# A modulation product moved from TensorE columns to VectorE half rows in a two-block transformer kernel

## The chip, the cores and the metric

One core of a Trainium2 chip runs the whole program. The metric is the device time of one execution in microseconds (us), as the median of several executions; lower is better. The engines of the core are called PE (TensorE, the matrix engine; PEld is its weight load), DVE (VectorE), ACT (ScalarE), POOL (GpSimd) and SP (SyncE, whose queue issues nearly all DMA transfers). Each engine executes its own list of instructions in order and waits for the others by semaphores.

## The reference, cut to what matters

The program computes two transformer blocks of two layers each, on 256 tokens with 1024 features; the first block also carries 256 context tokens through its first layer. In the first block each layer has an adaptive modulation: two condition vectors (`c` for the tokens, `c_ctx` for the context) give six vectors of 1024 numbers each, which shift, scale and gate what the layer does. The change concerns only this product, for the second layer (`l = 1`).

```python
for l in range(DEPTH):                                   # DEPTH = 2
    want_ctx = l < DEPTH - 1
    mod_x = jax.nn.silu(c) @ ada_w[l] + ada_b[l]         # ada_w[l]: 1024 x 6144, float32
    mod_c = jax.nn.silu(c_ctx) @ ada_w[l] + ada_b[l]
    sh1, sc1, g1, sh2, sc2, g2 = jnp.split(mod_x[:, None, :], 6, axis=-1)
    sh1c, sc1c, g1c, sh2c, sc2c, g2c = jnp.split(mod_c, 6, axis=-1)
    hx = rmsnorm(x, norm1_w[l]) * (1.0 + sc1) + sh1
    hc = rmsnorm(xc, norm1_w[l]) * (1.0 + sc1c) + sh1c
    mix_x, mix_c = token_mixers(hx, hc, ...)
    x = x + g1 * mix_x
    hx = rmsnorm(x, norm2_w[l]) * (1.0 + sc2) + sh2
    x = x + g2 * conv_ffn(hx, ...)
    if want_ctx:                                         # not in the last layer
        xc = xc + g1c * mix_c
        ...
```

In the second layer the context only enters through `sh1c` and `sc1c` (parts 0 and 1); its other four parts are not used.

## The kernel before

Features lie on the 128 partitions, tokens along the rows. A matrix of 1024 input features is cut into 8 blocks of 128 (`KD` = 8). Every large product is done with split operands: a float32 value is written as a rounded high part and a low part, and three matmuls (high-high, high-low, low-high; lines 414 to 416) give one block product. The weights arrive as 512 KB transfers of eight 128x128 blocks (`load`, line 344, five buffers in this stage); ACT rounds the high part (line 323), DVE subtracts to get the low part (line 307, tile `wl`), and four buffers of split weights stand between these two and PE.

The modulation of layer 1 is computed inside the feed-forward stage of layer 0 (`conv_ffn`), beside its matmuls. That stage has two halves. Each half first makes 11 pairs of up-projection products of 512 columns (`lin`, 8 blocks, 24 matmuls of 512 columns each; PE pays for two such products per pair), which ACT and DVE turn, by a short convolution, a Silu and a split (tiles `t`, `ah`, `al`), into the input of the down-projection; then 8 down-projection products of 11 blocks (33 matmuls), each followed by two DVE instructions that add into the residual (`residual`, line 724). Three accumulators in PSUM (tile `mm`) are used in turn.

Side work is cut into steps by Python generators. `queue(name, interval, depth, gens)` registers them; after each product `lin` calls `tick(us)` with the product's nominal time, `kt * 3 * columns / 2400` us (5.12 us for an up-projection, 7.04 us for a down-projection), and one step is taken for each `interval` of credit. `flush` takes all steps that are left. `soon()` raises the priority of what is traced in it, and `issue_after(ins)` puts instructions behind `ins` on its engine. From priorities and dependencies a scheduler fixes the order of every engine's instruction list when the program is built.

`ada_group` (line 595) is the generator for the modulation. One group covers 2048 of the 6144 columns. For each of 16 pieces it loads 512 KB (`araw`, one buffer, its transfer placed behind the last weight transfer) and does four matmuls with the two condition vectors as a stationary operand of 32 columns (line 605; float32, so each is two instructions, eight in all), which collect in four partition strips of one PSUM bank. At the end ACT copies the bank, PE transposes it in four pieces (line 614) and DVE adds the bias into `mod`. Layer 1 has three such groups, queued at an interval of 7.0 us at the start of the feed-forward stage of layer 0.

At the end of the stage comes a chain that PE waits for: the last residual, sums of squares over features (line 490), a power on POOL, a transposed spread (line 499), and `modnorm`, in which DVE, ACT and POOL make the input of layer 1. `warm` puts filler matmuls (line 369) into PE's wait.

Of the kernel before, what the change touches and what calls it, by code (L numbers as in the profile page):

```python
# [22 lines left out]
F32 = mybir.dt.float32  # L23
# [6 lines left out]
P = 128  # L30
D = 1024
# [257 lines left out]
class _K:  # L289
    def __init__(self, ctx, tc, a):  # L290
        self.ctx, self.tc, self.nc, self.a = ctx, tc, tc.nc, a
        self.queues = {}
        self.extra, self.wturn = None, [0, 0]
        self.last_load = None
        self.nsplit, self.held = 0, None
        self.last_mm = None
        self.ada1 = False

# [4 lines left out]
    def stt(self, out, in0, s, in1, op0, op1):  # L303
        self.nc.vector.scalar_tensor_tensor(out, in0, s, in1, op0=op0, op1=op1)  # L304

    def tt(self, out, in0, in1, op):
        self.nc.vector.tensor_tensor(out, in0, in1, op=op)  # L307
# [14 lines left out]
    def split(self, h, l, src):  # L322
        self.nc.scalar.copy(h, src)  # L323
        self.tt(l, src, h.bitcast(F32), OP.subtract)
# [201 lines left out]
    def setup(self):  # L526
# [23 lines left out]
        self.mod = [c.tile([P, 48, 2], F32, name=f"mod{l}") for l in range(DEPTH)]  # L550

# [68 lines left out]


# [22 lines left out]
    def modnorm(self, l, scale, part_shift, segs, xs, rb):  # L644

        shift = self.mod[l][:, part_shift * 8:(part_shift + 1) * 8, :]
        with self.soon():
            for k in range(KD):
# [10 lines left out]
                self.tt(xs[1][:, k, :nq], w, xs[0][:, k, :nq].bitcast(F32), OP.subtract)  # L659
# [13 lines left out]
    def block1(self, l, parts):  # L673
# [4 lines left out]
        with ExitStack() as lay:  # L678
# [7 lines left out]
            with ExitStack() as ph:  # L686
# [5 lines left out]
                else:  # L692
                    self.more_weights(ph, f"wm{l}", 0, 1)
                    rb = self.token_scale(parts)
                    if not self.ada1:
                        with tc.tile_pool(name="ada1", bufs=1) as ap:
                            for g in range(3):
                                for _ in self.ada_group(1, g, ap, 16):
                                    pass
# [8 lines left out]
            with ExitStack() as ph:  # L708
                self.more_weights(ph, f"wf{l}", 2, 2)
                if l == 0:  # L710
                    self.ada1 = True
                    self.queue("ada", 7.0, 1, *[self.ada_group(1, g, ada) for g in range(3)])
# [6 lines left out]
    def residual(self, ps, n, gate, l, segs, parts=None):  # L719

        g = self.mod[l][:, gate * 8:(gate + 1) * 8, :]
        for i, s in enumerate(segs):
            x = self.x[s][:, n, :]
            self.stt(x, ps[:, i * 256:(i + 1) * 256], g[:, n, 1 - s:2 - s], x, OP.mult, OP.add)
# [17 lines left out]
    def conv_ffn(self, l, st, xs, segs, nq):  # L742
# [8 lines left out]
        with tc.tile_pool(name=f"ffn{l}", bufs=1) as fp:  # L751
            for hf in range(halves):
                a_ = (fp.tile([P, nh, nq], F32R, name="ah"), fp.tile([P, nh, nq], F32R, name="al"))
                ready = []
                for jj in range(nh):
                    j = hf * nh + jj
                    if not ready:
                        banks = [self.tiles(nq) for _ in range(2 if hf + jj == 0 else G % 2 + 1)]
                        if hf + jj == 0:
                            self.lins(banks, st["wup"], xs, cols)  # L760
                        ready = [ps for bank in banks for ps in bank]
# [4 lines left out]
                    with self.soon():  # L766
# [13 lines left out]
                        self.split(a_[0][:, jj, :], a_[1][:, jj, :], v)  # L780
                parts = self.out(st["wdn"], a_, nh, 5, l, segs, hf == halves - 1)
        return parts
# [938 lines left out]
```

## Time and profile before

| | us |
|---|---|
| median of 3 runs | 3097.07 (3096.97 to 3097.26) |
| the profiled execution | 3097.39 |
| its span, first to last instruction | 3095.7 |
| PE busy | 3047.0 (98% of the span) |
| DVE busy | 1866.6 (60%) |
| ACT busy | 1468.1 (47%) |
| POOL busy | 405.5 (13%) |

The profile is of one execution. The share of busy time is an average over stages; what a change in one stage is worth is read from that stage. A "busy" matmul is pipelined with its neighbours, so the time that PE pays for it is the distance from its start to the next start, not its duration. "Idle before" an instruction is time in which its engine had nothing to run, with what ended it.

### The profile page before, as it was taken

Reading aid. Unit: us, or ns where it says so; the run is one execution under the profiler, and the core shown is the slowest. Engines: PE = TensorE matmul, PEld = TensorE weight load, DVE = VectorE, ACT = ScalarE, POOL = GpSimd, SP = SyncE. Lnnn points to the kernel's source line nnn. Section 1 sums busy time; section 2 is a strip of 40 time slices with the busy share of each in tenths; the row PEclk is TensorE's granted clock in tenths of the full one; section 3 lists DMA queues with packets and bytes.
Section 4 is the critical chain, followed back from the end, with each engine's and each line's share of the span. In section 5 each row is a group of like instructions: output and inputs, shape, how many; then the busy total and the mean of one; then the engine's idle time right before and its main releaser. Section 6 shows DMA issues by size and latency. Waiting matters only on the chain.

```text
span 3095.7 us, 52954 instructions
## 1 busy us (share of the span) xinstructions
PE 3047.0 (98%) x21412; PEld 2745.8 (89%) x21412; DVE 1866.6 (60%) x3064; ACT 1468.1 (47%) x2414; POOL 405.5 (13%) x419
## 2 busy tenths in 40 slices
PE   6999999999999999999999999999999999999999
PEld 4777878887777778899999999999999999999999
DVE  4467864336535546776587565576665665676664
ACT  4344463324323335455465444655544544654543
POOL 3212130112000033211100100122000000121000
PEclk9999999999999999999999999999999999999999
DMA  7423212324444423225555555444455554444553
GB/s 247 145 93 127 78 68 96 109 96 144 156 141 145 150 89 104 76 93 175 184 187 180 184 185 184 143 149 151 161 193 185 169 185 162 150 153 157 171 184 116
DMA packets 163429, 453.98 MB, mean 147 GB/s; under 512 B 14832, under 2 KB 66288, under 8 KB 162672
## 3 DMA queue, kind: packets, MB, share of 16 engines
q1 hardware_dynamic: 162464, 449.11, 43.9%
q8 instruction: 168, 2.75, 0.4%
q10 hardware_dynamic: 720, 1.49, 0.1%
q14 instruction: 77, 0.63, 0.1%
HBM read 447.13 MB, written 1.05 MB: 145 GB/s over the span
## 4 chain that ended last, share of the span: by engine, by line
PE 96%; DMA 1%; DVE 1%; ACT 1%; SPq 0%; issue 0%; POOL 0%; DVEq 0%; ACTq 0%; POOLq 0%
PE mm L414 25%; PE mm L416 25%; PE mm L415 25%; PE mm L436 2%; PE aux L605 2%; PE mm L437 2%; PE mm L435 2%; PE mm L428 1%; PE mm L429 1%; PE mm L427 1%; PE aux L1068 1%; DMA araw<-in_ada_dram 1%; PE aux L369 1%; PE aux L1569 1%; PE aux L1053 1%; PE aux L1043 1%
## 5 line engine op out<-in xcount | busy, mean ns | idle before, releaser
L307 DVE TENSOR_TENSOR wl<-raw,wh 128x1024 fp32r<-128x1024 f32 x746 | 922.2, 1239 | 780.9 <-ACT wh L323 763.0
L323 ACT CAST wh<-raw 128x1024 fp32r<-128x1024 f32 x746 | 782.5, 1051 | 1074.1 <-PE mm L415 736.4
L414 PE MATMUL mm<-xh,wh 128*128 128x256 f32 (+1 forms) x3680 | 1144.3, 311 | 4.2 <-ACT ao L301 3.0
L415 PE MATMUL mm<-xl,wh 128*128 128x256 f32 (+1 forms) x3680 | 1143.4, 311 | 0.0
L416 PE MATMUL mm<-xh,wl 128*128 128x256 f32 (+1 forms) x3680 | 1142.8, 311 | 0.0
L414 PEld LDWEIGHTS mm<-xh,wh 128*128 128x128 f32 x3680 | 699.3, 190 | 47.4 <-issue 8.4
L415 PEld LDWEIGHTS mm<-xl,wh 128*128 128x128 f32 x3680 | 699.5, 190 | 43.1 <-issue 9.6
L416 PEld LDWEIGHTS mm<-xh,wl 128*128 128x128 f32 x3680 | 699.3, 190 | 42.5 <-issue 7.5
L416 PE MATMUL mm<-ah,wl 128*128 128x256 f32 (+1 forms) x1056 | 317.5, 301 | 0.2 <-DVE wl L307 0.2
L415 PE MATMUL mm<-al,wh 128*128 128x256 f32 (+1 forms) x1056 | 317.6, 301 | 0.0
L414 PE MATMUL mm<-ah,wh 128*128 128x256 f32 (+1 forms) x1056 | 316.9, 301 | 0.0
L415 PEld LDWEIGHTS mm<-al,wh 128*128 128x128 f32 x1056 | 200.9, 190 | 9.1 <-issue 2.5
L416 PEld LDWEIGHTS mm<-ah,wl 128*128 128x128 f32 x1056 | 200.9, 190 | 9.1 <-issue 2.1
L414 PEld LDWEIGHTS mm<-ah,wh 128*128 128x128 f32 x1056 | 200.6, 190 | 8.7 <-issue 2.1
L310 POOL TENSOR_TENSOR small<-small,mhalf 128x2 f32<-128x2 f32 (+2 forms) x48 | 50.6, 1054 | 1051.7 <-DVE small L304 713.2
L310 POOL TENSOR_TENSOR ss<-ss,t 128x256 f32<-128x256 f32 (+1 forms) x68 | 72.1, 1061 | 623.7 <-ACT t L301 602.3
L304 DVE SCALAR_TENSOR_TENSOR cv<-glu,p,cv 128x512 f32<-128x512 f32 (+1 forms) x240 | 150.7, 628 | 3.5
L414 PE MATMUL mm<-bh,wh 128*128 128x512 f32 (+1 forms) x384 | 129.0, 337 | 1.3 <-ACT wh L323 0.7
L416 PE MATMUL mm<-bh,wl 128*128 128x512 f32 (+1 forms) x384 | 129.0, 337 | 0.3 <-DVE wl L307 0.3
L415 PE MATMUL mm<-bl,wh 128*128 128x512 f32 (+1 forms) x384 | 129.2, 337 | 0.0
L436 PE MATMUL mm<-wh,xl 128*128 128x256 f32 x448 | 127.8, 287 | 0.0
L437 PE MATMUL mm<-wl,xh 128*128 128x256 f32 x448 | 127.4, 286 | 0.0
(331 smaller groups left out, 4283.8 us busy)
## 6 DMA issues: line engine op xcount, KB each, us to landing
araw<-in_ada_dram SPq DMA_DIRECT2D x96, 512.0 KB, 3.9
raw<-in_a_wup_dram SPq DMA_DIRECT2D x88, 512.0 KB, 3.4
raw<-in_b_f1u_dram SPq DMA_DIRECT2D x88, 512.0 KB, 3.4
raw<-in_b_f2u_dram SPq DMA_DIRECT2D x88, 512.0 KB, 3.4
raw<-in_a_wi_dram SPq DMA_DIRECT2D x78, 512.0 KB, 3.3
raw<-in_b_wb_dram SPq DMA_DIRECT2D x72, 512.0 KB, 3.3
raw<-in_b_wi_dram SPq DMA_DIRECT2D x48, 512.0 KB, 3.4
raw<-in_a_wdn_dram SPq DMA_DIRECT2D x44, 512.0 KB, 3.3
```

Of the source, the lines that this page charges most:

```text
L304: self.nc.vector.scalar_tensor_tensor(out, in0, s, in1, op0=op0, op1=op1)
L307: self.nc.vector.tensor_tensor(out, in0, in1, op=op)
L310: self.nc.gpsimd.tensor_tensor(out, in0, in1, op=op)
L323: self.nc.scalar.copy(h, src)
L369: self.last_mm = self.nc.tensor.matmul(ps[0:32], x, x[:, 0:1].to_broadcast([P, 256]), start=True, stop=True).ins
L414: mm(ps, h, xh[:, k, cols], start=k == 0, stop=False)
L415: mm(ps, h, xl[:, k, cols], start=False, stop=False)
L416: self.last_mm = mm(ps, l, xh[:, k, cols], start=False, stop=k == kt - 1).ins
L435: mm(ps, xh, w[0], start=start, stop=False)
L436: mm(ps, xl, w[0], start=False, stop=False)
L437: mm(ps, xh, w[1], start=False, stop=stop)
L605: nc.tensor.matmul(ps[32 * j:32 * j + 32, c * 256:(c + 1) * 256], self.cpad[:, k, :], raw[:, j, :], start=k + c == 0, stop=k + c == KD)
```

## The change

The three groups of layer 1 are replaced by a generator `ada_parts`, which goes through the six parts of 1024 columns one after the other. For each block of 128 rows it loads 128x1024 numbers (512 KB, `arow`, four buffers, three transfers ahead), and DVE multiplies each row by the condition's value of that row and adds it to an accumulator of 128x1024, in two halves of 512. A part is closed by four PE transposes per half, a DVE sum along rows and the addition of the bias. The context's vector is done for parts 0 and 1 only; the rest of `mod` is set to zero once at the start. Each DVE instruction is placed behind the latest split or residual on DVE (`pace`). The generator is queued after the first up-projections, without raised priority, with an interval of 3.8 us during the up-projections and 1.4 us during the down-projections. The scratch pool `ada1` (four `arow`, two accumulators) is opened for the feed-forward stage. Layer 0 keeps `ada_group`.

```diff
@@ class _K
+        self.pace = None
     def stt(self, out, in0, s, in1, op0, op1):
-        self.nc.vector.scalar_tensor_tensor(out, in0, s, in1, op0=op0, op1=op1)
+        return self.nc.vector.scalar_tensor_tensor(out, in0, s, in1, op0=op0, op1=op1).ins
...
         self.mod = [c.tile([P, 48, 2], F32, name=f"mod{l}") for l in range(DEPTH)]
+        nc.gpsimd.memset(self.mod[-1], 0.0)
...
+    def ada_parts(self, l, parts, pool):
+        nc = self.nc
+        H = D // 2
+        src = [(part, k) for part in parts for k in range(KD)]
+        raws = {}
+
+        def fetch(i):
+            if i < len(src):
+                part, k = src[i]
+                raws[i] = pool.tile([P, D], F32, name="arow", bufs=4)
+                nc.sync.dma_start(raws[i], self.a["ada"][l, k * P:(k + 1) * P, part * D:(part + 1) * D])
+
+        for i in range(3):
+            fetch(i)
+        yield
+        for i, (part, k) in enumerate(src):
+            sets = (0,) if l == DEPTH - 1 and part > 1 else (0, 1)
+            if k == 0:
+                acc = [pool.tile([P, D], F32, name=f"aacc{w}") for w in sets]
+            fetch(i + 3)
+            for w in sets:
+                c = self.cpad[:, k, w:w + 1]
+                for h in (slice(0, H), slice(H, D)):
+                    with self.paced():
+                        if k == 0:
+                            self.ts(acc[w][:, h], raws[i][:, h], c, None, OP.mult)
+                        else:
+                            self.stt(acc[w][:, h], raws[i][:, h], c, acc[w][:, h], OP.mult, OP.add)
+                    yield
+            del raws[i]
+            if k < KD - 1:
+                continue
+            for w in sets:
+                m = self.mod[l][:, part * KD:(part + 1) * KD, w]
+                for h in range(2):
+                    pt = self.aux()
+                    for j in range(4):
+                        nc.tensor.transpose(pt[:, j * P:(j + 1) * P], acc[w][:, h * H + j * P:h * H + (j + 1) * P], self.ident)
+                    t = self.small(4)
+                    with self.paced():
+                        nc.vector.tensor_reduce(t, pt.rearrange("p (j n) -> p j n", j=4), axis=AX.X, op=OP.add)
+                        self.tt(m[:, h * 4:h * 4 + 4], t, self.par(l, "adab")[:, part * KD + h * 4:part * KD + h * 4 + 4], OP.add)
+                    yield
+
+    def paced(self):
+        return self.tc.issue_after(self.pace) if self.pace else nullcontext()
@@ modnorm
-                self.tt(xs[1][:, k, :nq], w, xs[0][:, k, :nq].bitcast(F32), OP.subtract)
+                self.pace = self.tt(xs[1][:, k, :nq], w, xs[0][:, k, :nq].bitcast(F32), OP.subtract)
@@ block1
-                    self.queue("ada", 7.0, 1, *[self.ada_group(1, g, ada) for g in range(3)])
+                    self.adap = ph.enter_context(tc.tile_pool(name="ada1", bufs=1))
@@ residual
-            self.stt(x, ps[:, i * 256:(i + 1) * 256], g[:, n, 1 - s:2 - s], x, OP.mult, OP.add)
+            self.pace = self.stt(x, ps[:, i * 256:(i + 1) * 256], g[:, n, 1 - s:2 - s], x, OP.mult, OP.add)
@@ conv_ffn
                             self.lins(banks, st["wup"], xs, cols)
+                            if l == 0:
+                                self.queue("ada", 3.8, 1, self.ada_parts(1, range(6), self.adap), early=False)
...
-                        self.split(a_[0][:, jj, :], a_[1][:, jj, :], v)
+                        self.pace = self.split(a_[0][:, jj, :], a_[1][:, jj, :], v)
+                if l == 0:
+                    self.queue("ada", 1.4, 1)
                 parts = self.out(st["wdn"], a_, nh, 5, l, segs, hf == halves - 1)
+                if l == 0:
+                    self.queue("ada", 3.8, 1)
```

## Rows read from the trace of the kernel before

**Rows 1.** The page: busy time of each engine, granted clock, DMA rate by slice.
```profile
PE 3047.0 (98%) x21412; PEld 2745.8 (89%) x21412; DVE 1866.6 (60%) x3064; ACT 1468.1 (47%) x2414; POOL 405.5 (13%) x419
...
GB/s 247 145 93 127 78 68 96 109 96 144 156 141 145 150 89 104 76 93 175 184 187 180 184 185 184 143 149 151 161 193 185 169 185 162 150 153 157 171 184 116
```
**Rows 2.** Stage sums: window, its length, busy us (x instructions), clock, DMA share, GB/s.
```profile
730.00:864.00 134.00, 134.00 (x662) 100.99 (x660) 79.95 (x107) 56.72 (x77) 10.85 (x13) 1.00 0.45 149
864.00:931.00 67.00, 67.00 (x333) 50.84 (x332) 22.28 (x30) 13.83 (x15) 0.00 (x0) 1.00 0.49 157
931.00:1064.00 133.00, 133.00 (x652) 100.71 (x651) 70.92 (x90) 49.48 (x64) 0.00 (x0) 1.00 0.45 146
1064.00:1131.00 67.00, 67.00 (x337) 50.76 (x335) 21.70 (x33) 18.26 (x28) 8.46 (x6) 1.00 0.37 119
```
**Rows 3.** Waits in 728 to 1131 us: engine, line, waited-for, total us, times, longest.
```profile
ACT wh L323 <- PE mm L415: 174.6, 59, 6.3
DVE wl L307 <- ACT wh L323: 114.5, 52, 5.0
```
**Rows 4.** One group of instructions in 728 to 1131 us: busy us, mean ns, idle before.
```profile
L605 PE MATMUL aux<-araw,cpad 128*32 128x256 f32 x380 | 32.9, 391 | 0.0
```
**Rows 5.** PE in order of time, 774 to 782 us: start, us, instruction.
```profile
774.78 0.39 PE L416 MATMUL mm<-xh,wl 128*128 128x512 f32 x1
...
778.18 0.39 PE L416 MATMUL mm<-xh,wl 128*128 128x512 f32 x1
...
779.31 0.39 PE L415 MATMUL mm<-xl,wh 128*128 128x512 f32 x1
...
779.63 0.64 PE L605 MATMUL aux<-araw,cpad 128*32 128x256 f32 x8
...
780.20 0.50 PE L416 MATMUL mm<-xh,wl 128*128 128x512 f32 x1
...
781.46 0.40 PE L415 MATMUL mm<-xl,wh 128*128 128x512 f32 x1
```
**Rows 6.** PE in order of time around the transposes that close a group.
```profile
1129.02 0.39 PE L414 MATMUL mm<-ah,wh 128*128 128x512 f32 x1
...
1129.25 0.60 PE L614 MATMUL aux<-cst,t 128*128 128x128 f32 x4
...
1130.62 0.39 PE L416 MATMUL mm<-ah,wl 128*128 128x512 f32 x1
```
**Rows 7.** DVE groups of the whole span: shape, count, busy us, mean ns.
```profile
L304 DVE SCALAR_TENSOR_TENSOR cv<-glu,p,cv 128x512 f32<-128x512 f32 x120 | 91.4, 761 | 1.3
...
L995 DVE TENSOR_REDUCE small<-aux 128x1 f32<-128x512 f32 x32 | 21.8, 681 | 13.3 <-PE aux L1043 13.2
...
L304 DVE SCALAR_TENSOR_TENSOR bl<-merged,bh 128x512 fp32r<-128x512 f32 x8 | 5.0, 686 | 2.1 <-ACT bh L301 2.1
...
L307 DVE TENSOR_TENSOR mod<-aux,p 128x8 f32<-128x8 f32 x24 | 2.3, 159 | 20.0 <-PE aux L614 20.0
```
**Rows 8.** The transfers of the modulation's weights in 728 to 1131 us.
```profile
DMA to landing us min/median/max: 3.5/3.8/6.5
```
**Rows 9.** The SP queue's own waits in 728 to 1131 us.
```profile
SPq L344 <- DVE wl L307: 212.7, 56, 10.6
```
**Rows 10.** DVE in order of time during the up-projection, idle before in brackets.
```profile
782.90 0.69 DVE L307 TENSOR_TENSOR t<-t,t 128x512 f32<-128x512 f32 x1 [0.76 <-ACT t L301]
784.28 0.69 DVE L307 TENSOR_TENSOR al<-t,ah 128x512 fp32r<-128x512 f32 x1 [0.69 <-ACT ah L323]
785.71 1.22 DVE L307 TENSOR_TENSOR wl<-raw,wh 128x1024 fp32r<-128x1024 f32 x1 [0.73 <-ACT wh L323]
...
791.94 1.23 DVE L307 TENSOR_TENSOR wl<-raw,wh 128x1024 fp32r<-128x1024 f32 x1 [3.57 <-DMA araw<-in_ada_dram]
```
**Rows 11.** DVE in order of time at the end of the stage.
```profile
1133.20 0.16 DVE L316 TENSOR_SCALAR small<-aux 128x4 f32<-128x4 f32 x1 [1.28 <-PE aux L490]
1135.28 0.42 DVE L307 TENSOR_TENSOR t<-xc,aux 128x256 f32<-128x256 f32 x1 [1.92 <-PE aux L499]
```

More of the change, by code (lines that the diff above doesn't have):

```diff
@@ L303, in stt @@
     def stt(self, out, in0, s, in1, op0, op1):
-        self.nc.vector.scalar_tensor_tensor(out, in0, s, in1, op0=op0, op1=op1)
+        return self.nc.vector.scalar_tensor_tensor(out, in0, s, in1, op0=op0, op1=op1).ins
     def tt(self, out, in0, in1, op):
-        self.nc.vector.tensor_tensor(out, in0, in1, op=op)
+        return self.nc.vector.tensor_tensor(out, in0, in1, op=op).ins
     def ptt(self, out, in0, in1, op):
@@ L323, in split @@
         self.nc.scalar.copy(h, src)
-        self.tt(l, src, h.bitcast(F32), OP.subtract)
+        return self.tt(l, src, h.bitcast(F32), OP.subtract)
     def more_weights(self, stack, name, raw, parts):
@@ L696, in block1 @@
                         with tc.tile_pool(name="ada1", bufs=1) as ap:
-                            for g in range(3):
-                                for _ in self.ada_group(1, g, ap, 16):
-                                    pass
+                            for _ in self.ada_parts(1, range(6), ap):
+                                pass
                 self.modnorm(l, self.mod_scale(l, 1, "n1", f"sc1_{l}"), 0, [0, 1], xs, rb)
```

## The prediction

> **What bounds the kernel now.** I read the page first: PE is busy 98% of its span [rows 1], so time can only be won where PE works on something that can go, or where it waits. Next I summed the engines over the four passes of layer 0's feed-forward stage, which is where the change lies (up, down, up, down, at 730, 864, 931 and 1064 us): PE is busy for all of every pass at clock 1.00, while DVE is busy 79.95 of 134, 22.28 of 67, 70.92 of 133 and 21.70 of 67 us, together 194.8 of 401 [rows 2]. The list of waits for 728 to 1131 us has no entry of PE at all; what waits there is ACT for PE to free a buffer of split weights, 174.6 us, and DVE for ACT behind it, 114.5 us [rows 3]. So in this stage each us of PE's list is a us of the program, and DVE, ACT and the loads run ahead of PE and are held back by it. The same was asked of single instructions in order of time, below.
>
> **What is removed from PE.** A matmul of 512 columns is paid by the distance of starts: from 774.78 to 778.18 us lie 15 of them, 3.40 / 15 = 0.2267 us each [rows 5]. One piece of the modulation (four float32 matmuls, eight instructions) stands between the matmuls of 779.31 and 780.20; the matmul of 781.46 is the sixth after that of 779.31. Six distances without the piece would be 1.36 us, it took 2.15, so a piece costs 0.79 us, although its eight instructions show only 0.64 [rows 5]. There are 48 pieces (3 groups of 16). The records show 380 instructions in the window, some 47 pieces [rows 4]; the first starts at its edge, in the chain at the start of the stage, and I price it at nothing: 47 x 0.79 = 37.1 us. A group's four closing transposes: from 1129.02 to 1130.62 us lie five distances, 1.60 us against 5 x 0.2267 = 1.13, so 0.47 [rows 6], three times 1.4 us. Removed: 38.5 us. As a cross-check from the code: 44 up-projections of 24 matmuls and 16 down-projections of 33 are 1584 matmuls, at 0.2267 us 359.1 us; the four passes take 401 [rows 2], which leaves 41.9 us, and 38.5 of it is now named.
>
> **What is added to PE.** Four transposes close each half of a part: parts 0 and 1 have two vectors, parts 2 to 5 one, so 2 x 2 x 2 + 4 x 2 = 16 closings. They are the same shape as line 614, 0.47 us each in the stream [rows 6]. Of these, how many fall beside the matmuls? Steps follow credit: the first half's ten up-projection pairs after the queue is set give 102.4 us at 3.8, 26 steps; its eight down-projections 56.3 us at 1.4 with the remainder, 42; the second half 29 and 42. That is 139. The generator needs 1 + 128 + 16 = 145 steps, so six remain for the flush: four products and part 5's two closings, in the chain between the layers, whose 3.4 us PE cannot use for matmuls of the next layer [rows 11]. In the stream: 14 x 0.47 = 6.6 us. The two others are bounded by 0 and 0.9 us.
>
> **What is added to DVE, and what covers it.** 128 products of 128x512. No row has this instruction with both tensors contiguous and accumulating in place; the nearest is line 304 of `bl`, the same operation on 512 contiguous float32, 0.686 us; the row with a strided operand, 0.761, is the upper end [rows 7]. Sixteen of them are a plain product, taken at the same price. Each closing adds a sum over 512 numbers out of PSUM, 0.681, and a small addition, 0.159 [rows 7]. 128 x 0.686 + 16 x 0.84 = 87.8 + 13.4 = 101.2 us; with 0.761 it is 110.8. Off go twelve additions, 1.9 us. DVE then has 194.8 + 99 = 294 us of work in 401 - 38.5 + 6.6 = 369 us, 80%. By pass the heaviest is the last: 42 steps, of which 38 products and four closings, 29.4 us, on 21.7, 51 of some 60 us (8 x 33 x 0.2267). It fits, so the cover is DVE's own idle time: the gaps of 0.76, 0.69, 0.73 and 3.57 us between its steps [rows 10]. If a product ends up in front of a split, the split starts up to 0.69 us late. Behind it stand ACT's next split, four buffers, of some 5.4 us of matmuls each, ahead of PE; the wait of ACT on PE, 6.3 us at the longest [rows 3], is what such a delay eats first. The accumulators in PSUM are three, so a late convolution step has one more product's time, 5.4 us. I put both at nothing on PE. ACT loses three copies, POOL gains one fill at the start; neither engine ends a wait of PE here [rows 3].
>
> **The loads.** The bytes stay: 48 transfers of 512 KB. They landed in 3.5 to 6.5 us, 3.8 in the middle [rows 8], and are now asked for three blocks ahead. Each now waits on SP's queue for DVE to release a buffer, and weight transfers stand behind it. Those already wait for DVE, 212.7 us over 56 times, up to 10.6 at a stretch, without PE noticing [rows 9]: price nothing. But the rate changes: the last pass takes about 19 of the 48 blocks (38 products at two a block) in 60 us, 10 MB, with 88 blocks of weights (8 products of 11 blocks, 64 KB each), 5.8 MB, so some 263 GB/s, where the passes now show 119 to 157 [rows 2] and the fastest slice of the page, at the start, 247 [rows 1]. That no row shows; it is rival three.
>
> **The end of the stage.** DVE has gaps of 1.28 and 1.92 us between the last residual and `modnorm` [rows 11]. Four products and two closings left over are 4 x 0.69 + 2 x 0.84 = 4.4 us against 3.2 us of gaps. In the best case they cost nothing (raised priority lets the chain pass), in the worst all 4.4; I take 1, nearer to the gaps.
>
> **Waits at the closings.** A closing stands in PE's list where the scheduler thought DVE done. If DVE is late, PE waits. Nothing in the rows shows such a pair, PE waits for nobody here [rows 3]. Bounds: 0, and one split [rows 10] with one product in front, 1.23 + 0.69 = 1.9 us, times 14 = 27 us. With one vector a half's last product is two steps before its closing, with two vectors four; I take 0.15 us each, 2 us.
>
> **Sum**, on the profiled execution, 3097.39: - 38.5 + 6.6 + 1 + 2 = - 28.9, so 3068.5. The median lies 0.3 us below the profiled time: 3068.
>
> **Rivals.** *Two: closings and splits that come late.* DVE at 80% or more, with five steps given out at once after each down-projection, makes PE wait 1 us or more at most closings, or the order puts products in front of convolution steps. For it: the last pass at 51 of 60 us. Against it: no wait of PE in 400 us now. At 1 us for each of 14, 3068 - 2 + 14 = 3080; at the bound of 1.9, 3093, which is no change. *Three: slower, by starved products.* DVE runs in order, so a product that waits for its transfer holds the splits behind it. DVE's slack is 369 - 294 = 75 us, 1.6 us per block. Above that DVE sets the time. The gain of 29 us is gone when waits reach 104 us, 2.2 us per block, and from there it is slower; at the landing of 3.8 us, if asked for only when needed, 48 x 3.8 = 182 us of waits give 3068 + 182 - 75 = 3175, and at 3 us 3137. For it: the rate of the last pass. The Trainium skill, in "DMA: Bandwidth & Descriptors", section "Latency and other measured facts", says that a memory access goes from 0.2 us to 2 us at high load; by that, an estimate, a landing would take 1.8 us longer, and no row here shows it. Against it: the lead of two blocks, some 6 us in the last pass and 15 us and more in the first, is above the median landing of 3.8 [rows 8]. *Four: it does not free PE*, because the pieces ran in time PE could not use. Against it: PE busy 401 of 401 us [rows 2], and 0.79 us seen in the distances. It would give 3097 + 7 + 3 = 3107, slower; hardly to be believed.
>
> **How the numbers follow.** The forecast, 3068, with DVE prices at either end and the end of the stage and the closings between 0 and 10 us, holds from 3061 (3064.4 with all added work but the transposes hidden and the first piece won too, less the 3.4 us of the cross-check that are not named) to 3078: 0.70. Rival two up to 3090: 0.15, and from there to no change: 0.07. Rival three: 0.06, four: 0.02. A measurement of this kernel can tell about 0.2%, 6.2 us, from no change: faster is below 3090.9. Faster 0.85, same 0.07, slower 0.08. The range runs from 3061 to 3089, through most of rival two; it leaves out some 0.17 above and 0.02 below.
>
> **What would show it.** In the changed profile: no line 605 after 730 us; the four passes together some 32 us shorter; 64 transposes of the new line in 16 groups, without idle time of PE before them; DVE busy some 295 us over the stage, products at 0.69 us; ACT still waiting for PE, not the other way. Wrong would be: PE waiting for DVE at the closings or for `wl` (rival two), DVE idle before products with a transfer as the end of it (three), passes as long as before (four), or, at the end of the stage, more than the 3.4 us that now lie between DVE's last residual (1133.20 less the idle 1.28) and `modnorm`'s first instruction at 1135.28 [rows 11].

## The result: 31 us of 3097, and where they came from

| kernel | median us (range) | kernel before beside it | ratio, 95% interval |
|---|---|---|---|
| changed | 3066.01 (3064.59 to 3067.86) | 3097.02 | 0.99 (0.9888 to 0.9913) |
| changed, run again later | 3067.59 (3065.39 to 3069.71) | 3096.06 | 0.9909 (0.9892 to 0.9925) |

The changed kernel is 1% faster, 3066 us where 3068 was forecast. Its profiled execution took 3065.65 us, with a span of 3063.9. The page gives the same share of PE as before on a span that is 31.8 us shorter [rows 1]; DVE has 91 us more work:

```profile
PE 3009.1 (98%) x21080; PEld 2744.1 (90%) x21080; DVE 1957.3 (64%) x3212; ACT 1461.0 (48%) x2411; POOL 410.1 (13%) x420
```

So I go to the stage again, from the first up-projection matmul of layer 0 to the first of layer 1. Before, its four passes began at 730.07, 864.39, 930.63 and 1064.14 us and layer 1 at 1137.03; after, the same matmuls stand at 728.38, 849.39, 911.09, 1033.55 and 1107.18:

| us | up | down | up | down, and the way to layer 1 | stage |
|---|---|---|---|---|---|
| before | 134.3 | 66.2 | 133.5 | 72.9 | 407.0 |
| after | 121.0 | 61.7 | 122.5 | 73.6 | 378.8 |

28.2 of the 31.8 us of span are in this stage. Of the rest, 1.7 lie before it (the first piece of the modulation, in the chain at its start, among them) and 1.9 behind it, where kernels with the same code vary by more. The first three passes gained 28.8 us together; the last one, with the way to layer 1 behind it, gained nothing. The sums of the passes show it too. Columns are as in [rows 2], and the fifth window is the way from the last down-projection to layer 1, in the changed kernel:

```profile
728.50:849.50 121.00, 120.29 (x530) 98.97 (x529) 94.32 (x128) 55.66 (x78) 11.32 (x14) 1.00 0.39 126
849.50:911.20 61.70, 61.70 (x282) 51.21 (x281) 48.63 (x76) 13.42 (x15) 0.00 (x0) 1.00 0.55 174
911.20:1033.60 122.40, 122.40 (x554) 101.50 (x553) 87.79 (x122) 48.84 (x64) 0.00 (x0) 1.00 0.45 144
1033.60:1095.00 61.40, 61.40 (x280) 50.92 (x279) 51.00 (x76) 17.48 (x27) 13.65 (x6) 1.00 0.64 214
1095.00:1107.30 12.30, 9.02 (x63) 8.08 (x62) 7.22 (x17) 2.21 (x5) 4.38 (x14) 0.86 0.14 44
```

PE is still busy for the whole of the passes, but for 0.7 us at the start of the first, a wait for ACT. DVE is busy 94 of 121, 49 of 62, 88 of 122 and 51 of 61 us: 281.7 of 366.5, 77%, against 49% before. The last window is the new thing: PE busy 9.0 of 12.3 us, at a granted clock of 0.86, where all others have 1.00. The waits of 728 to 1110 us name the place:

```profile
ACT wh L324 <- PE mm L416: 139.9, 52, 6.1
DVE wl L308 <- ACT wh L324: 44.2, 40, 3.8
...
PE aux L662 <- DVE aacc L305: 3.0, 1, 3.0
```

ACT still waits for PE (139.9 us, 174.6 before [rows 3]), so PE still sets the pace of the passes. DVE's waits for ACT's splits fell from 114.5 to 44.2 us: this idle time is the larger part of what the products filled. PE waits for a closing (line 662) once, 3.0 us, and that is in the last window.

What was added, by groups of DVE's instructions in 728 to 1110 us (count, busy us, mean ns):

```profile
L305 DVE SCALAR_TENSOR_TENSOR aacc<-arow,cpad,aacc 128x512 f32<-128x512 f32 x112 | 80.9, 771 | 0.0
...
L665 DVE TENSOR_REDUCE small<-aux 128x4 f32<-128x512 f32 x16 | 10.6, 685 | 7.4 <-PE aux L662 7.4
...
L315 DVE TENSOR_SCALAR aacc<-arow,cpad 128x512 f32<-128x512 f32 x16 | 7.7, 515 | 0.0
```

The products kept DVE busy for 80.9 + 7.7 = 88.6 us, 87.8 forecast, but by errors that cancel. An accumulating product shows 0.771 us in the mean and not 0.686, a plain one 0.515; 112 of the one and 16 of the other add up to 94.6. Products that follow one another overlap (four take 2.73 us in the block below, 0.66 from start to start), and so the busy time is 6 us less than that sum. The sums along rows are as priced, 0.685 against 0.681 [rows 7].

A closing in the stream, PE in order of time:

```profile
870.47 0.39 PE L415 MATMUL mm<-ah,wh 128*128 128x512 f32 x1
870.70 0.60 PE L662 MATMUL aux<-cst,aacc 128*128 128x128 f32 x4
...
872.53 0.40 PE L416 MATMUL mm<-al,wh 128*128 128x512 f32 x1
```

The matmul of 872.53 is the seventh after that of 870.47; seven distances of 0.2267 are 1.59 us [rows 5], they took 2.06, so the closing costs 0.47, and no idle time stands before it. Fourteen closings lie in the passes: 0, 4, 6 and 4 of them. And the end of the stage, PE in order of time; in brackets is the idle time before an instruction, and what ended it:

```profile
1095.00 0.39 PE L417 MATMUL mm<-ah,wl 128*128 128x512 f32 x1
...
1098.35 1.91 PE L662 MATMUL aux<-cst,aacc 128*128 128x128 f32 x8 [2.95 <-DVE aacc L305]
...
1101.12 2.20 PE L491 MATMUL aux<-cst,ss 128*128 128x1 f32 x16
...
1104.68 0.65 PE L500 MATMUL aux<-cst,small 128*128 128x128 f32 x4 [0.33 <-POOL small L311]
...
1107.18 0.63 PE L428 MATMUL mm<-xh,wh 128*128 128x512 f32 x2
```

From the last down-projection matmul (1095.00) to the first of layer 1 (1107.18) are 12.2 us; before, from 1130.62 [rows 6] to 1137.03, 6.4:

```profile
1137.03 0.63 PE L427 MATMUL mm<-xh,wh 128*128 128x512 f32 x2
```

The two closings left for the flush stand in PE's list ahead of the sums of squares of line 491, which the norm needs. DVE at that time:

```profile
1095.83 0.47 DVE L305 SCALAR_TENSOR_TENSOR xx<-mm,mod,xx 128x256 f32<-128x256 f32 x1
1096.22 2.73 DVE L305 SCALAR_TENSOR_TENSOR aacc<-arow,cpad,aacc 128x512 f32<-128x512 f32 x4
...
1099.44 0.69 DVE L665 TENSOR_REDUCE small<-aux 128x4 f32<-128x512 f32 x1 [0.49 <-PE aux L662]
...
1105.44 0.42 DVE L308 TENSOR_TENSOR t<-xc,aux 128x256 f32<-128x256 f32 x1 [1.92 <-PE aux L500]
```

Four products left over, 2.73 us, in one block right behind the last residual (`xx`); PE stands still for them. From the end of that residual, 1096.30, to the first instruction of `modnorm`, 1105.44, are 9.1 us, where 3.4 lay before [rows 11]: this is the sign of being wrong that the prediction named for the end of the stage. PE's clock is lower for a while after its stop. Windows of 1 us, columns as in [rows 2]:

```profile
1099.00:1100.00 1.00, 1.00 (x7) 0.93 (x6) 0.56 (x1) 0.00 (x0) 0.00 (x0) 0.50 0.00 0
1100.00:1101.00 1.00, 1.00 (x7) 0.81 (x6) 0.95 (x3) 0.00 (x0) 0.68 (x2) 0.50 0.00 0
```

The granted clock is 0.50, the lower of its two levels (1.2 GHz), from 1099 to 1101 us, and 1.00 from 1102 on: most of the eight transposes run in that stretch.

### The profile page after: what moved, and what is told of

Its sections match the earlier page's. It is cut to its first block, busy times and chain, and to the rows that moved or that the text cites. A ratio compares the mean times of both kernels' runs of the same rounds, so it can differ in the third digit from the quotient of the medians.

```text
span 3063.9 us, 52478 instructions
## 1 busy us (share of the span) xinstructions
PE 3009.1 (98%) x21080; PEld 2744.1 (90%) x21080; DVE 1957.3 (64%) x3212; ACT 1461.0 (48%) x2411; POOL 410.1 (13%) x420
## 4 chain that ended last, share of the span: by engine, by line
PE 96%; DVE 1%; DMA 1%; ACT 1%; SPq 0%; issue 0%; POOL 0%; DVEq 0%; ACTq 0%; POOLq 0%
PE mm L415 26%; PE mm L417 26%; PE mm L416 25%; PE mm L437 2%; PE mm L438 2%; PE mm L436 2%; PE mm L429 1%; PE mm L430 1%; PE mm L428 1%; PE aux L1125 1%; PE aux L607 1%; DMA araw<-in_ada_dram 1%; PE aux L370 1%; PE aux L1626 1%; PE aux L1110 1%; PE aux L1100 1%
```

## The experiments

The stage is the sharper measure in what follows: kernels start it at 728.4 to 731.1 us, and the rest of the span behind it varies between 1954.0 and 1961.7, so a total scatters by 2 or 3 us, while stages of the same code agree within 0.5.

### No second-layer modulation at all

The kernel leaves the product out, and the modulation of layer 1 stays zero.

```diff
-                                self.queue("ada", 3.8, 1, self.ada_parts(1, range(6), self.adap), early=False)
+                                pass
 ...
-                if l == 0:
-                    self.queue("ada", 1.4, 1)
 ...
-                if l == 0:
-                    self.queue("ada", 3.8, 1)
```

> Layer 1's modulation is left out altogether (its vector stays zero): no pieces, no products, no closings. What it measures is the removal by itself. The theory of the prediction, that every microsecond of PE in this stage is one of the program: 3097.0 less 47 pieces of 0.79 us and three times 0.47 us (38.5), so 3058.5, and down to 3055 if the first piece (0.6 us in the chain ahead of the stage) and the 3.4 us that the cross-check left unnamed go too. The change as made would then have paid 7 to 11 us for what it adds. Rival: the pieces partly lay in time that PE could not use, then it stays above 3062.

Measured: 3056.46 us (3054.28 to 3059.35) beside 3096.16, ratio 0.9872 (0.9858 to 0.9887), within the 3055 to 3058.5 expected. The stage takes 366.1 us (120.6, 59.8, 119.7, 66.0), 40.8 less than before. This is what the pieces and transposes of the old modulation cost, priced at 38.5. The difference is most of the 3.4 us that the cross-check could not name. A place in the trace of before shows part of it, where a group's closing transposes (line 614) are mixed with a piece of the next group:

```profile
860.18 0.39 PE L416 MATMUL mm<-xh,wl 128*128 128x512 f32 x1
860.41 0.38 PE L614 MATMUL aux<-cst,t 128*128 128x128 f32 x2
860.72 0.62 PE L605 MATMUL aux<-araw,cpad 128*32 128x256 f32 x2
...
862.89 0.50 PE L414 MATMUL mm<-xh,wh 128*128 128x512 f32 x1
```

2.71 us lie between the two matmuls, 2.5 more than their pitch, where a piece (0.79) and the transposes (0.47) were priced at 1.26. Two of the three groups end like this, so 2 x 1.23 = 2.5 us of the 3.4 are here.

The passes also price the closings in the stream by themselves: after less this kernel is 0.4, 1.9, 2.8 us for the first three passes, with 0, 4 and 6 closings: 4.7 us for ten, 0.47 each, as taken from [rows 6]. The 0.4 without a closing is scatter: the first pass of one and the same kernel, below, took 121.0 us in one run and 120.5 in another. The last pass with the way to layer 1 differs by 7.6 us, of which four closings explain 1.9. So 5.7 us go at the end of the stage.

### No step left for the end

The steps are given out a little faster, so that all 145 fall beside matmuls.

```diff
-                                self.queue("ada", 3.8, 1, self.ada_parts(1, range(6), self.adap), early=False)
+                                self.queue("ada", 3.4, 1, self.ada_parts(1, range(6), self.adap), early=False)
 ...
-                    self.queue("ada", 1.4, 1)
+                    self.queue("ada", 1.25, 1)
 ...
-                    self.queue("ada", 3.8, 1)
+                    self.queue("ada", 3.4, 1)
```

> The changed kernel with intervals of 3.4 and 1.25 us in place of 3.8 and 1.4, so that all 145 steps are taken before the last down-projection's tick and none is left for the flush. Theory: the end of the stage grew by 5.8 us (12.2 us from the last down-projection matmul to the first of layer 1, 6.4 before) because the two last closings stand in PE's list ahead of the sums of squares and wait for four products on DVE. With nothing left it is 6.4 again: 3066.0 - 5.8 + 2 x 0.47 = 3061. Rival, that DVE's higher load in the last pass is what delays the end: then the higher rate makes it no shorter, 3066 or more.

Measured: 3063.09 us (3061.85 to 3065.76), ratio 0.9894 (0.988 to 0.9909); the stage takes 374.0 us (121.0, 62.9, 121.3, 68.8), 4.8 less than the changed kernel. PE at the end of the stage, in order of time:

```profile
1097.03 0.39 PE L417 MATMUL mm<-ah,wl 128*128 128x512 f32 x1
...
1097.37 0.95 PE L491 MATMUL aux<-cst,ss 128*128 128x1 f32 x8
...
1100.93 0.65 PE L500 MATMUL aux<-cst,small 128*128 128x128 f32 x4 [0.33 <-POOL small L311]
...
1103.44 0.63 PE L428 MATMUL mm<-xh,wh 128*128 128x512 f32 x2
```

The way to layer 1 is 6.4 us, as before the change. From line 491's first matmul to line 500 are 3.56 us here and 3.56 in the changed kernel, so all of the 5.8 us lies ahead of line 491: 0.34 us here from the last down-projection matmul to it, 6.12 there, of which 2.95 are the idle time and 2.77 the stretch from 1098.35, with the transposes at the lower clock. All 16 closings are in the stream now, which costs 2 x 0.47 more there and takes 5.8 off at the end. The floor for this form of the change is the kernel without modulation plus 16 closings, 366.1 + 7.5 = 373.6 us: with all closings in the stream, little is left to win by moving steps. The same kernel, with the next set of runs:

> The version with earlier steps (3.4 and 1.25 us) once more, on another chip: 3061 to 3065, 3 to 4 us under the changed kernel; the stage 374.0 us.

Measured: 3062.90 us (3060.04 to 3064.56), ratio 0.9892 (0.9878 to 0.9907); stage 373.5 us, 120.5 in the first pass and again 68.8 in the last. By its own totals it is 2.9 to 4.7 us ahead of the changed kernel, about what the scatter of totals allows one to see; by the stage, 4.8 and 5.3. No version that computes the modulation was faster.

### The norm's sums ahead of the closings left over

```diff
                 parts = self.conv_ffn(l, st, xs, segs, nq)
+                if l == 0:
+                    self.rb1 = self.token_scale(parts)
 ...
-                    rb = self.token_scale(parts)
+                    rb = self.rb1
```

> The changed kernel with its intervals, but the sums of squares and the spread for layer 1 are traced before the flush of the six left-over steps, so that they stand ahead of the two last closings in PE's list; DVE has the same four products left. Theory (order in PE's list): the chain falls to some 7 us, 3061. Rival (DVE's left-over work itself fills the chain, 4.4 us of it): stays at 3065 or more.

Measured: 3068.02 us (3067.93 to 3068.43), ratio 0.991 (0.9893 to 0.9926). The stage is 374.4 us, 4.4 less, with the leftover steps still there, but the total is no shorter, as the rival had it. PE in order of time:

```profile
1097.04 0.95 PE L491 MATMUL aux<-cst,ss 128*128 128x1 f32 x8
...
1101.66 0.65 PE L500 MATMUL aux<-cst,small 128*128 128x128 f32 x4 [1.37 <-POOL small L311]
...
1104.16 0.60 PE L662 MATMUL aux<-cst,aacc 128*128 128x128 f32 x4
...
1115.26 0.50 PE L429 MATMUL mm<-xl,wh 128*128 128x512 f32 x1 [2.75 <-DVE xl L308]
```

The sums of line 491 no longer wait for products, and the closings run behind line 500, the second of them (1105.06) already among layer 1's matmuls. But PE now waits for the normalised input `xl` of layer 1, since the closings' sums along rows and additions stand among the instructions of `modnorm` in DVE's list. One of these additions, 0.155 us in the mean in the changed kernel, took 1.94:

```profile
1111.10 1.94 DVE L308 TENSOR_TENSOR mod<-small,p 128x4 f32<-128x4 f32 x1
```

So the stage ends too early to be the measure here. The distance from the last down-projection matmul to the first matmul of 256 columns in layer 1, with the same 72 matmuls of layer 1 ahead of that one in each kernel, shows it:

| us from the last down-projection matmul | to layer 1 | to the first matmul of 256 columns |
|---|---|---|
| before | 6.4 | 24.9 |
| changed | 12.2 | 30.4 |
| no step left for the end | 6.4 | 24.9 |
| the norm's sums first | 7.8 | 30.4 |

The 4.4 us that were gained before layer 1 are lost again within its first 23 us. The leftover steps cost 5.5 us in either order, once by PE's list and once by DVE's; only with none left over does the cost go. The span behind the stage is 5.0 us longer than in the changed kernel (1961.7 against 1956.7), and 4.4 of it are this.

### Without the pace rule

Every product may start as soon as its block is loaded.

```diff
     def paced(self):
-        return self.tc.issue_after(self.pace) if self.pace else nullcontext()
+        return nullcontext()
```

> The changed kernel without the rule that a product stands behind the latest split or residual on DVE. If the rule protects the splits and the convolution steps, PE now waits for them in the passes: 3070 or more. If DVE's lead over PE is long enough by itself (ACT waited 140 us for PE over this stage in the changed kernel), nothing changes: 3064 to 3068.

Measured: 3094.09 us (3092.24 to 3099.11) beside 3096.16, ratio 0.9994 (0.9985 to 1.0004). 28 of the 31 us are gone. The stage takes 405.7 us: 154.0, 59.8, 120.6, 71.2. The whole loss is in the first pass, 33 us. It now holds 38 of the 64 closing transposes (at 0.47 us for four, some 4.5 of the 33 us), and the other passes, with 0, 8 and 18, are shorter than with the rule. The first 80 us of that pass, columns as in [rows 2]:

```profile
730.00:770.00 40.00, 24.76 (x89) 17.56 (x88) 40.00 (x69) 13.28 (x22) 17.99 (x16) 0.83 0.46 149
770.00:810.00 40.00, 34.55 (x147) 28.35 (x148) 40.00 (x64) 12.85 (x17) 0.00 (x0) 0.87 0.66 207
```

DVE is busy for 80 us without a gap and PE for 59 of them, at a lower clock. The waits of the pass show for what:

```profile
PE mm L415 <- DVE t L305: 10.7, 2, 9.5
PE mm L429 <- DVE xl L308: 9.5, 7, 3.3
```

PE waits for the convolution's steps and for the normalised input, which stand on DVE behind products that nobody needs yet. DVE is busy for as long over the whole span (1957.7 us, 1957.3 with the rule). The order alone turns a gain into no change.

### The pace rule at the start only

The rule is kept where `modnorm` sets `self.pace`, and not renewed by splits and residuals.

```diff
-            self.pace = self.stt(x, ps[:, i * 256:(i + 1) * 256], g[:, n, 1 - s:2 - s], x, OP.mult, OP.add)
+            self.stt(x, ps[:, i * 256:(i + 1) * 256], g[:, n, 1 - s:2 - s], x, OP.mult, OP.add)
 ...
-                        self.pace = self.split(a_[0][:, jj, :], a_[1][:, jj, :], v)
+                        self.split(a_[0][:, jj, :], a_[1][:, jj, :], v)
```

> The products are held behind the normalisation at the start of the stage only; splits and residuals no longer move that mark. It tells apart where the unpaced kernel lost its 33 us of the first up pass: if the loss comes from products pulled ahead of the normalisation, this is as fast as the changed kernel, 3064 to 3068. If it comes from products put in bulk ahead of splits and convolution steps all along, the first pass is still 8 us or more longer than in the changed kernel (121 us): 3074 to 3090.

Measured: 3087.40 us (3084.36 to 3088.13), ratio 0.997 (0.9958 to 0.9981). The first pass takes 148.2 us: of the 33 us that are lost without any rule 27 are lost here too, with no product ahead of the norm. Twelve closings, 5.6 us, are among them; the rest is PE waiting or at a lower clock (0.94 in the mean). The pass holds 100 of the 128 products, where it holds 25 in the changed kernel. DVE in order of time shows how:

```profile
755.28 0.74 DVE L305 SCALAR_TENSOR_TENSOR t<-mm,p,t 128x510 f32<-128x510 f32 x1
755.94 2.07 DVE L305 SCALAR_TENSOR_TENSOR aacc<-arow,cpad,aacc 128x512 f32<-128x512 f32 x3
757.92 0.75 DVE L305 SCALAR_TENSOR_TENSOR t<-mm,p,t 128x510 f32<-128x510 f32 x1
758.58 3.40 DVE L305 SCALAR_TENSOR_TENSOR aacc<-arow,cpad,aacc 128x512 f32<-128x512 f32 x5
```

Between two steps of one convolution (`t<-mm,p,t`) stand three products, and five behind the second. The convolution frees the accumulator that PE needs next, and PE had waited 9.8 us for one when it started at 756.17.

### Twice the products for the parts that need one vector

The generator makes both vectors for all parts, 192 products and 24 closings instead of 128 and 16, given out faster in proportion. The extra results aren't read.

```diff
-            sets = (0,) if l == DEPTH - 1 and part > 1 else (0, 1)
+            sets = (0, 1)
 ...
-                                self.queue("ada", 3.8, 1, self.ada_parts(1, range(6), self.adap), early=False)
+                                self.queue("ada", 2.5, 1, self.ada_parts(1, range(6), self.adap), early=False)
 ...
-                    self.queue("ada", 1.4, 1)
+                    self.queue("ada", 0.915, 1)
 ...
-                    self.queue("ada", 3.8, 1)
+                    self.queue("ada", 2.5, 1)
```

> Both condition vectors for all six parts (64 more products, 8 more closings), with intervals cut to 2.5 and 0.915 us so that about as many steps are left for the flush. DVE gets 64 x 0.75 + 8 x 0.84 = 55 us more, 92% of the stage. Theory (DVE has 75 us of slack, its order keeps the splits in time): only the closings are paid, 8 x 0.47 = 3.8, and one more in the flush: 3070 +- 2. Rival (DVE near its limit delays PE): each down pass, where DVE would be busy 70 of 61 us, becomes DVE's: 9 us in each of two, 3085 or more.

Measured: 3077.29 us (3074.64 to 3078.24), ratio 0.9938 (0.9924 to 0.9953). Stage 389.3 us: 122.9, 61.7, 123.5, 81.2. 64 more products in the passes cost PE no more than their closings: the first three passes grew by 1.9, 0.0 and 1.0 us. The last, with the way to layer 1, grew by 7.6, and there PE waits at three closings:

```profile
1102.23 0.83 PE L662 MATMUL aux<-cst,aacc 128*128 128x128 f32 x4 [3.40 <-DVE aacc L305]
...
1104.34 1.08 PE L662 MATMUL aux<-cst,aacc 128*128 128x128 f32 x4 [1.27 <-DVE aacc L305]
...
1106.92 1.09 PE L662 MATMUL aux<-cst,aacc 128*128 128x128 f32 x4 [1.50 <-DVE aacc L305]
```

The products that DVE could not place in its gaps pile up and are paid at the end, where no matmul stands beside them. Both expectations were off: the lower had no such backlog, and the higher had it in both down-projections.

### Blocks asked for one ahead instead of three

```diff
-                raws[i] = pool.tile([P, D], F32, name="arow", bufs=4)
+                raws[i] = pool.tile([P, D], F32, name="arow", bufs=2)
 ...
-        for i in range(3):
+        for i in range(1):
 ...
-            fetch(i + 3)
+            fetch(i + 1)
```

> Two row buffers and one transfer ahead in place of four and three. A transfer lands in 4.3 us; in the last pass a block lasts about 3 us, so each product pair there waits 1 to 2 us. Theory (DVE's slack covers waits up to 1.6 us a block on average): some 30 blocks x 2 = 60 us of waits, covered, the time stays at 3064 to 3070. Rival (a product that waits for its transfer holds the splits, and PE waits): 3080 or more.

Measured: 3072.19 us (3071.08 to 3074.75), ratio 0.9924 (0.991 to 0.9939), above the 3070 expected at most. Stage 384.0 us: 120.6, 61.7, 122.5, 79.3. The waits of the stage:

```profile
DVE aacc L305 <- DMA arow<-in_ada_dram: 11.2, 10, 3.0
...
PE aux L662 <- DVE aacc L305: 8.7, 1, 8.7
```

Here is rival three at a small price: DVE waits for transfers ten times, 11.2 us, and not one of these is felt in the first three passes. The last pass pays 5.6 us, at the one closing where PE waited 3.0 before. To see whether the wait moves away with the leftover steps, the same with the faster steps of the second experiment:

> Earlier steps (3.4 and 1.25 us) with two row buffers and one transfer ahead. Theory (a product that waits for its transfer costs PE nothing in the passes; it only makes work spill over the end of the stage, where the closings stand ahead of the sums): with the steps taken earlier there is room, and most of the 5.7 us that two buffers cost with the later steps is gone: the stage 374 to 376 us, 3062 to 3066. Rival (the waits cost in the passes once these are fuller): 3068 or more.

Measured: 3065.57 us (3064.67 to 3068.98), ratio 0.9906 (0.9889 to 0.9922); stage 377.9 us (121.0, 62.9, 121.3, 72.7), 3.9 to 4.4 over the same with four buffers. I expected most of what two buffers cost to go, 5.2 us of the stage; 0.8 to 1.3 did. DVE waits 15.1 us for transfers, in twelve times, and PE waits 3.0 us at two closings, now within the last pass. So late closings in the stream, rival two, do exist once transfers are late; with four buffers they didn't appear. Loading ahead is worth 4 to 5 us here.

### Whole rows instead of half rows

One product of 128x1024 in place of two of 128x512, every second step then being empty.

```diff
-                        if k == 0:
-                            self.ts(acc[w][:, h], raws[i][:, h], c, None, OP.mult)
+                        if h.start:
+                            pass
+                        elif k == 0:
+                            self.ts(acc[w], raws[i], c, None, OP.mult)
                         else:
-                            self.stt(acc[w][:, h], raws[i][:, h], c, acc[w][:, h], OP.mult, OP.add)
+                            self.stt(acc[w], raws[i], c, acc[w], OP.mult, OP.add)
```

> The changed kernel with one product of 128x1024 where it has two of 128x512, given out at the first of the two steps. DVE has 64 instructions of some 1.3 us (the split of 128x1024 takes 1.24, the pointer operand adds some 0.06) in place of 128 of 0.75: 13 us less work. Theory (DVE has slack, and its order is held by the mark): the three first passes as long as in the changed kernel within 0.5 us; the end changes by what is left over, 3063 to 3068. Rival (the half rows matter, because a split or a convolution step behind a whole row comes too late): the up passes grow by 2 us or more each, 3070 or more.

Measured: 3067.14 us (3064.72 to 3069.45), ratio 0.9909 (0.9893 to 0.9926); stage 378.9 us, the changed kernel's 378.8. And with the faster steps:

> Earlier steps and whole rows together. DVE has slack, so whole rows add nothing to PE: within 1.5 us of the version with earlier steps, 3061 to 3065, the stage 374 us. If whole rows delay splits, 3066 or more.

Measured: 3063.13 us (3062.72 to 3063.43), ratio 0.9894 (0.9879 to 0.9909); stage 373.9 us, against 374.0 and 373.5 with half rows. A whole-row product takes 1.277 us in the middle against 2 x 0.743; DVE's busy time falls from 80.9 us for 112 accumulating halves to 73.5 for 56 rows, 0.13 us a pair, but nothing on PE's path changes. The division into half rows, which the change is named after, is worth nothing measurable.

The changed kernel was run once more, beside the kernels with the rule at the start only, with all vectors and with two buffers:

> The changed kernel once more, unaltered, beside the next three on one chip: 3064 to 3068, and the stage (first matmul of layer 0's up-projections to the first of layer 1) 378.8 us as before within 0.5.

Measured: as in the first table; stage 378.8 us, pass by pass the same to 0.1.

## Why the prediction was right, step by step

| step | priced, us | measured, us | by what |
|---|---|---|---|
| removed from PE | 38.5 | 40.8 | stage before less stage without modulation |
| closings in the stream, 14 | 6.6 | 6.5 | first three passes, 4.65 for 10; last by the same |
| waits at those closings | 2 (0 to 27) | 0 | waits of PE in the passes |
| end of the stage | 1 (0 to 4.4) | 5.8 | 12.2 less 6.4; no step left for the end |
| net in the stage | -28.9 | -28.2 | 378.8 less 407.0; the terms give -28.5 |

**The bound.** That PE's list is the time of these passes was right: PE busy for all of each pass, before and after, and each closing is seen in the passes at its price. Rival four is dead by the kernel without modulation.

**Removed.** Right in mechanism, 2.3 us too small. The distance of starts was taken at a piece that stands alone; at two group ends pieces and transposes are mixed, and cost twice the sum of their prices there.

**Products under cover.** Right: all but the last four products (2.7 of 88.6 us) stand in the passes, and none made PE wait there. The price of one was taken from the wrong row. `bl` of line 304 has a constant as its scalar; the product has one number for each partition, from `cpad`, and so has `cv` in the same [rows 7], which I took for the upper end because its operand is strided. The kernel before has another row with a constant, in place and with plain float32 out, and it takes no longer than `bl`:

```profile
L304 DVE SCALAR_TENSOR_TENSOR cv<-aux,cv 128x512 f32<-128x512 f32 x4 | 2.5, 684 | 2.3 <-PE aux L1114 2.3
```

The kind of the scalar is what goes with the price in these rows; no run changes it alone. The product's middle was 0.743 and its mean 0.771. Plain products were 0.480 in the middle instead of the same 0.686, and products in a row overlap, so the sum came out right by luck. The Trainium skill, in "VectorE: DVE Perf Modes", section "The perf-mode tier table (the rule you actually need)", gives such a one-source product on float32 in SBUF twice the rate of an operation on two tensors. The trace agrees in what further columns cost, not in the whole time: from half rows to whole rows the plain product grows by 0.266 us (0.480 to 0.746), the accumulating one by 0.534 (0.743 to 1.277), while at 512 columns they stand at 0.480 and 0.743.

**What the cover rests on.** I named DVE's idle time, and left out that the order has to be enforced. Without the pace rule DVE has the same work and 28 of the 31 us are gone. I had put a product in front of a split at up to 0.69 us, and nothing on PE; without the rule up to six of them lie between one step of the convolution and the next, step after step. Rival two names this order in half a sentence, but its prices, 1 to 1.9 us, are for the 14 closings alone: that DVE's order, not its capacity or its transfers, makes it the bound of one pass has no price there, and it cost 33 us.

**The end of the stage.** Mis-sized, and outside its own bounds: 1 us was taken, 0 to 4.4 allowed, and 5.8 measured. I compared 4.4 us of DVE's work with 3.2 us of DVE's gaps, and in the best case had the chain pass the leftover work. In PE's list the two closings stand ahead of line 491, so the norm's sums wait for four products and for eight transposes, and those gaps come only after that. Giving all steps out earlier takes the 5.8 us away, which shows the size. With the sums put first the cost moves into layer 1, by DVE's list, and is as large at the first matmul of 256 columns: that the chain can pass the leftover steps for nothing was wrong for both lists.

**Rivals two and three.** Neither happened with four buffers. The last pass moved 214 GB/s, and the blocks landed in 4.3 us in the middle, 3.6 to 6.4 (3.5 to 6.5 and 3.8 before [rows 8]), under the lead that three blocks give. With two buffers both appear, at 4 to 6 us in sum.

**By chance or not.** The terms missed by -2.3, -0.1, -2 and +4.8 us, which add up to +0.4. The forecast is right by its mechanism and its large term; that it is within 2 us is in part because the smaller errors cancel. The 3.6 us of span outside the stage (1.7 before it, 1.9 behind) are in no term but for the first piece, which was priced at nothing.

## What to carry to other kernels

Work moved off a full engine can be hidden in a second one, here up to 77% busy with it, if an order keeps it behind what the full engine will need next: here that order was worth 28 of 31 us, and the idle time alone almost nothing. Do not leave steps over for the end of a stage: six of them cost 5.8 us, and a place further back in one engine's list only moved the cost to another's. Follow such a gain past the end of the stage before believing it. When a price is taken from a near row, match the kind of its scalar operand as well as its shape.

## What the hardware showed that was not expected

**Some of DVE's products take longer beside POOL.** The middle of the accumulating products is 743 ns, but three of 112 took 1.77 to 1.78 us. The view of one tile's instructions (min, middle, max in ns, then first and last start in us, and the transfers' landing):

```profile
L305 DVE SCALAR_TENSOR_TENSOR aacc<-arow,cpad,aacc x112: 733/743/1784, 770.6 to 1098.2; 128x512 f32<-128x512 f32 x112
L315 DVE TENSOR_SCALAR aacc<-arow,cpad x16: 475/480/1054, 752.1 to 1083.2; 128x512 f32<-128x512 f32 x16
...
DMA to landing us min/median/max: 3.6/4.3/6.4
```

All three start while POOL adds squares (`ss`), at 1060.23, 1070.96 and 1090.07. POOL in order of time:

```profile
1059.11 2.35 POOL L311 TENSOR_TENSOR ss<-ss,t 128x512 f32<-128x512 f32 x1 [5.16 <-ACT t L302]
1067.84 4.34 POOL L311 TENSOR_TENSOR ss<-ss,t 128x512 f32<-128x512 f32 x1 [6.38 <-ACT t L302]
```

The same addition took 1.28 to 1.67 us in this stage before the change; now it takes up to 4.34 (1.88 around 1090.07), by spans that are rough on POOL. Not every product beside it is slow: the three that start at 1067.84, 1068.50 and 1069.16, within the longest addition, and the one at 1089.40 took 0.74, so first POOL was late and then the next product. The whole-row products show it too, 1.277 us in the middle and 2.2 to 2.3 beside an addition of POOL. It cost nothing here, since PE did not wait. The Trainium skill, in "GPSIMD Engine Reference", section "1. Specifications", says that POOL shares its ways into SBUF with DVE and contends with DVE instructions that read two tensors there; the trace agrees, and the runs add the size, a factor of 2.4 on DVE and of up to 2.6 on POOL (4.34 / 1.67).

**The clock fell after some short stops.** PE's idle 2.95 us at the end of the stage were followed by some 3 us at the lower level of the granted clock, and there the eight transposes took 1.91 us (four take 0.60 in the stream). The kernel with products for both vectors waited 3.40, 1.27 and 1.50 us in a row, and its clock stood at 0.50 from 1103 to 1115 us. With the norm's sums first, idle times of 1.37 us (before line 500) and 2.75 us (before the matmul of 1115.26) left it at 1.00. It also stood at 0.50 for some 3 us just ahead of the stage, from 726 us on, in the run with whole rows and in that with two buffers, where PE ran fillers and the norm's sums and had been idle for 0.3 us at most; so a stop is not all that it follows, and the rule stays open. A stop of PE cost more than its own length here: 5.8 us for 2.95 of waiting and for transposes that cost 2 x 0.47 in the stream, some 1.9 us more than the two.
